# Matmul with subtraction on one core: runs of 16 m tiles, 36 longer transfers, an eighth VectorE pair, shared semaphores, and the last wait behind the section's exit

## Chip, cores, metric

One core of one Trainium2 chip. The metric is the device time of one execution in microseconds (us); a kernel's time is the median of its runs. Most of the argument is about the span that the profiler sees, some 1.8 us shorter than the time, and about moments in it, counted from its start.

## The reference

```python
batch, m, k, n = 16, 512, 1024, 768          # x [16,512,1024], weight [1024,768], sub_value [16,512,768], float32
def reference(x, weight, sub_value):
    return (np.matmul(x, weight) - sub_value).astype(np.float32)
```

That is 64 m tiles of 128 rows. Bytes to move: x 33.6 MB, weight 3.1, sub_value 25.2, output 25.2, together 87.03 MB.

## The kernel before

ScalarE casts a tile of x to fp16; PE transposes it (as pairs of fp16 in one 32-bit word), ScalarE evacuates the transpose, and PE multiplies it with the weight; VectorE subtracts in place in the ring that holds sub_value, from which the output leaves. For seven pairs of tiles VectorE transposes instead of PE. One queue (SP) issues all transfers, in the order of a list. A list entry is kind, first m tile, number of m tiles; `x` loads x, `s` sub_value, `w` a quarter of the weight, `o` stores output.

```python
S = 8                                       # m tiles in a run
NX, NSO = 16, 32                            # slots in the ring of x, in the ring of sub_value/output
ON_DVE = frozenset(range(18, 60, 6))        # first tiles of the pairs that VectorE transposes
TRANSFERS = [
    ('x', 0, 1), ('w', 0, 1), ('x', 1, 1), ('w', 1, 1), ('x', 2, 1), ('w', 2, 1),
    ('w', 3, 1), ('x', 3, 2), ('s', 0, 1), ('x', 5, 3), ('s', 1, 3), ('x', 8, 3),
    ('s', 4, 4), ('x', 11, 5), ('s', 8, 8), ('x', 16, 8), ('x', 24, 3), ('s', 16, 8),
    # ... cut ...
    ('x', 56, 8), ('s', 56, 8), ('o', 32, 8), ('o', 40, 8), ('o', 48, 8), ('o', 56, 4),
    ('o', 60, 2), ('o', 62, 1), ('o', 63, 1),
]
# partition p of a run holds S rows that follow each other, one for each m tile:
x_s = x_flat.rearrange("(s p j) k -> s p j k", p=P, j=S)
# ... cut: in issue(), for each entry once its waits can be named ...
sem = tc.alloc_semaphore(f"{kind}{at}")     # a semaphore for each transfer
sp.add(lambda here=here, there=there: nc.sync.dma_start(out=here, in_=there), waits, (sem, 16))
# ... cut: at the end, inside the section that all engines run in ...
for t in range(n_mt):
    if t == 0 or landed["o", t] is not landed["o", t - 1]:
        nc.sync.wait_ge(landed["o", t], 16)
```

A transfer that takes n m tiles of a run moves n consecutive rows for each of the 128 partitions; neighbouring partitions lie S rows apart in memory.

Of the kernel before, what the change touches and what calls it, by code (L numbers as in the profile page):

```python
# [10 lines left out]
F32 = mybir.dt.float32  # L11
F16 = mybir.dt.float16

S = 8
NX, NSO = 16, 32
N16, NXT, NPT, NPO = 4, 5, 2, 3
N16P, NXTP = 2, 2
# [2 lines left out]
LEAD_DVE = 7  # L20
PER = 4
HEAD = 3
ON_DVE = frozenset(range(18, 60, 6))
LOOP = None

TRANSFERS = [
    ('x', 0, 1), ('w', 0, 1), ('x', 1, 1), ('w', 1, 1), ('x', 2, 1), ('w', 2, 1),
    ('w', 3, 1), ('x', 3, 2), ('s', 0, 1), ('x', 5, 3), ('s', 1, 3), ('x', 8, 3),
    ('s', 4, 4), ('x', 11, 5), ('s', 8, 8), ('x', 16, 8), ('x', 24, 3), ('s', 16, 8),
    ('x', 27, 5), ('o', 0, 8), ('s', 24, 8), ('x', 32, 8), ('s', 32, 8), ('o', 8, 8),  # L30
    ('x', 40, 8), ('s', 40, 8), ('x', 48, 8), ('o', 16, 8), ('o', 24, 8), ('s', 48, 8),
    ('x', 56, 8), ('s', 56, 8), ('o', 32, 8), ('o', 40, 8), ('o', 48, 8), ('o', 56, 4),
    ('o', 60, 2), ('o', 62, 1), ('o', 63, 1),
]


# [66 lines left out]
def kernel(  # L103
# [7 lines left out]
    nc = tc.nc  # L111
# [7 lines left out]
    n_mt = M_TOT // P  # L119
# [3 lines left out]

    x_s = x_flat.rearrange("(s p j) k -> s p j k", p=P, j=S)
    sub_s = sub_flat.rearrange("(s p j) n -> s p j n", p=P, j=S)
    out_s = out_flat.rearrange("(s p j) n -> s p j n", p=P, j=S)
    w_c = weight.rearrange("(c p r) n -> c p r n", p=P, r=2)

    ctx.enter_context(tc.tile_critical(no_gpsimd_drain=True))  # L129

    def sbuf(name, shape, dtype):
        return ctx.enter_context(nc.sbuf_tensor(name, shape, dtype)).ap()
# [18 lines left out]
    counter = {}  # L151
# [4 lines left out]
    def count(name):  # L156
        so_far[name] += 1
        return (counter[name], 1)
# [23 lines left out]
    landed = {}  # L182
    cast_at, evac_at, pair_at, turn_at, mul_at, finish_at, w_at = {}, {}, {}, {}, {}, {}, {}
# [4 lines left out]
    def take(pool_name, n, mi):  # L188

        b = used[pool_name] % n  # L190
        used[pool_name] += 1
        slot[pool_name, mi] = b
        before = holder.get((pool_name, b))
        holder[pool_name, b] = mi
        return b, before
# [3 lines left out]
    todo = list(TRANSFERS)  # L199
    done = {"w": set(), "x": set(), "s": set(), "o": set(), "cast": set(), "finish": set()}  # L200
    staged = {}

    def issue():
        while todo:
            kind, at, n = todo[0]
            span = set(range(at, at + n))
            old = {t - NX if kind == "x" else t - NSO for t in span}
            need, by = {
                "w": (set(), "o"),
                "x": ({t for t in old if t >= 0}, "cast"),  # L210
                "s": ({t for t in old if t >= 0}, "o"),
                "o": (span, "finish"),
            }[kind]
            if not need <= done[by]:
                return
            todo.pop(0)
            done[kind] |= span
            sem = tc.alloc_semaphore(f"{kind}{at}")
            if kind == "w":

                first = NSO - 2 * (n_c - at)
                st = so_ring[:, first : first + 2]
                sp.add(lambda st=st, at=at: nc.sync.dma_start(out=st, in_=w_c[at]), then=(sem, 16))  # L223
                for r in range(2):
                    dve.add(
                        lambda at=at, r=r, st=st: nc.vector.tensor_copy(out=w_sb[:, at, r], in_=st[:, r]),  # L226
                        waits=[(sem, 16)], then=count("w"),
                    )
                    staged[first + r] = so_far["w"]
                w_at[at] = so_far["w"]  # L230
                continue
            ring, size, view = {
                "x": (x_ring, NX, x_s), "s": (so_ring, NSO, sub_s), "o": (so_ring, NSO, out_s)
            }[kind]
            here = ring[:, at % size : at % size + n]
            there = view[at // S][:, at % S : at % S + n]
            waits = []
            if kind == "x" and need:
                waits.append((counter["cast"], max(cast_at[t] for t in need)))
            if kind == "s":  # L240
                for t in need:
                    waits.append((landed["o", t], 16))
                for t in span:
                    if t % NSO in staged:
                        waits.append((counter["w"], staged.pop(t % NSO)))
            if kind == "o":
                waits.append((counter["finish"], max(finish_at[t] for t in need)))
            for t in span:
                landed[kind, t] = sem
            if kind == "o":  # L250
                here, there = there, here
            sp.add(lambda here=here, there=there: nc.sync.dma_start(out=here, in_=there), waits, (sem, 16))  # L252

    def cast(mi):
        assert mi in done["x"]
        done["cast"].add(mi)
        x_in = x_ring[:, mi % NX]
        first = mi - mi % 2
        waits = [(landed["x", mi], 16)]
        if first in ON_DVE:  # L260
            if mi == first:
                b, before = take("x16p", N16P, mi)
                if before is not None:
                    waits.append((counter["pair"], pair_at[before]))
            to = x16p_b[:, slot["x16p", first], mi - first]
        else:
            b, before = take("x16", N16, mi)
            if before is not None:
                waits.append((counter["turn"], turn_at[before]))
            to = x16_b[:, b]  # L270
        act.add(lambda: nc.scalar.copy(out=to, in_=x_in), waits, count("cast"))  # L271
        cast_at[mi] = so_far["cast"]
        issue()
# [27 lines left out]
    def transposes_dve(mi):  # L301

        x16 = x16p_b[:, slot["x16p", mi]].bitcast(F32).rearrange("p j (c q) -> p (j c) q", c=n_c)
        blocks = [(a, b) for a in range(P // Q) for b in range(P // Q)]

        def one(n, a, b):
            def f():
                waits = []
                if n == 0:
                    d, before = take("xtp", NXTP, mi)  # L310
                    waits.append((counter["cast"], cast_at[mi + 1]))
                    if before is not None:
                        waits.append((counter["mul"], mul_at[before + 1]))
                xt = xtp_b[:, slot["xtp", mi]].bitcast(F32).rearrange("p j (c m) -> p (j c) m", c=n_c)
                last = n == len(blocks) - 1
                dve.add(lambda: nc.vector.transpose(  # L316
                    xt[b * Q : (b + 1) * Q, :, a * Q : (a + 1) * Q],
                    x16[a * Q : (a + 1) * Q, :, b * Q : (b + 1) * Q],
                ), waits, count("pair") if last else None)
                if last:  # L320
                    pair_at[mi] = so_far["pair"]
            return f
        return [one(n, a, b) for n, (a, b) in enumerate(blocks)]

    def matmuls(mi, c):
        first = mi - mi % 2
        on_dve = first in ON_DVE
        waits = []
# [26 lines left out]
    def finish(mi):  # L355
        assert mi in done["s"]
        done["finish"].add(mi)
        o = so_ring[:, mi % NSO].rearrange("p (h n) -> p h n", h=2)
        po = po_b[:, slot["po", mi]]
        dve.add(lambda: nc.vector.tensor_tensor(  # L360
            out=o, in0=po[:, :, :NS], in1=o, op=mybir.AluOpType.subtract
        ), [(landed["s", mi], 16), (counter["mul"], mul_at[mi])], count("finish"))
        finish_at[mi] = so_far["finish"]
        issue()

# [15 lines left out]
    def lead(mi):  # L381
        return LEAD_DVE if mi - mi % 2 in ON_DVE else TA + CA

# [8 lines left out]
    idle(5)  # L392
    matmuls(0, 0)
    cast(1)
    transpose_tile(1)
    idle(4)
# [25 lines left out]
    for mi in range(HEAD, n_mt):  # L422
# [3 lines left out]
        t = mi + TA  # L426
        tr = transposes(t) if t < n_mt and t - t % 2 not in ON_DVE else []
        for c in range(n_c):
# [6 lines left out]
        finish(mi)  # L435
        if mi + LEAD_DVE - 1 in ON_DVE:
            waiting += transposes_dve(mi + LEAD_DVE - 1)
# [5 lines left out]

    for q in (sp, act, dve, pool):
        q.emit(q.ops)
    for t in range(n_mt):
        if t == 0 or landed["o", t] is not landed["o", t - 1]:
            nc.sync.wait_ge(landed["o", t], 16)
    if LOOP:
        first, size, times = LOOP  # L450
        pe.emit(pe.ops[: marks[first]])
        ends = [marks[first + size * n] for n in range(times + 1)]
        pe.emit_loop([pe.ops[a:b] for a, b in zip(ends, ends[1:])])
        pe.emit(pe.ops[ends[-1] :])
    else:
        pe.emit(pe.ops)


# [28 lines left out]
```

## Time and profile before

| | before |
|---|---|
| time, median of the first four runs | 211.37 us (211.04 to 211.59) |
| span of the profiled run | 209.36 us |
| PE busy / DMA engines busy | 95% / 97.8% |
| PE's last matmul ends | 204.41 us |
| eighth transfer (x3, x4) landed on all engines | 17.55 us |
| last output landed | 207.74 us |
| from there to the end of the span | 1.62 us |

The last four rows are read from the trace's instruction and landing times. One view more is needed later, the waits of PE from 24.3 us on. Its columns are: who waited, for whom, us in total, times, the longest.

```profile
PE po_b L175 <- ACT xt_b L296: 1.5, 1, 1.5
PE pt_b L289 <- ACT x_b L271: 1.4, 1, 1.4
PE po_b L175 <- DVE xtp_b L316: 0.3, 1, 0.3
```

The wait of the first line is at 57 us (that of the second ended at 24.1 us, as the window begins): the cast of tile 18 stands in ScalarE's order and waits for x16 to x23, which land at 56.56 us; the evacuation that PE needs stands behind it. So a late load shows as PE waiting for ScalarE.

### The profile page before, as it was taken

How to read it: one execution, taken by the hardware profiler on the slowest of the kernel's cores; microseconds unless marked ns; L12 is line 12 of the kernel's file. 1: busy time of each engine (PE TensorE's matmuls, PEld its weight loads, DVE VectorE, ACT ScalarE, POOL GpSimd, SP SyncE). 2: the span in 40 equal slices, each digit the busy share in tenths (PEclk: the TensorE clock that was granted, in tenths of full speed). 3: DMA queues.
4: the chain of work that ended last, by engine and by line, in shares of the span. 5: the costliest groups of instructions: out<-in, count | busy, mean ns of one | idle time of the engine just before them, and what ended most of it. 6: DMA issues, size and time to landing. Idle time of an engine off the chain costs nothing.

```text
span 209.4 us, 2456 instructions
## 1 busy us (share of the span) xinstructions
PE 198.4 (95%) x1250; PEld 80.4 (38%) x738; DVE 114.0 (54%) x186; ACT 112.9 (54%) x115; POOL 0.7 (0%) x6
## 2 busy tenths in 40 slices
PE   7998799999979999999999999999999999999990
PEld 2432244444333344344344334434434433444430
DVE  0242235106149849929956965992994795332231
ACT  2555665676396274655727629455572750765410
POOL 1000000000000000000000000000000000000000
PEclk9999999999999999999999999999999999999998
DMA  6999999999999999999999999999999999999994
GB/s 200 417 427 425 427 432 434 441 438 423 401 448 417 452 412 429 452 432 424 421 427 452 415 437 448 407 424 446 423 435 441 426 423 426 427 434 432 427 383 171
DMA packets 5626, 87.17 MB, mean 416 GB/s; under 512 B 624, under 2 KB 624, under 8 KB 2032
## 3 DMA queue, kind: packets, MB, share of 16 engines
q1 hardware_dynamic: 5616, 87.03, 97.8%
q8 instruction: 7, 0.11, 0.2%
q14 instruction: 3, 0.02, 0.0%
HBM read 61.87 MB, written 25.17 MB: 416 GB/s over the span
## 4 chain that ended last, share of the span: by engine, by line
PE 80%; DMA 6%; DVE 5%; ACT 4%; SPq 2%; issue 1%; ACTq 0%
PE po_b L175 71%; PE pt_b L289 10%; DMA x_ring<-in_x_dram 6%; DVE xtp_b L316 3%; ACT x_b L271 2%; ACT xt_b L296 1%; DVE so_ring L360 1%; SPq L223 1%; SPq L252 1%; ACT x16p_b L271 0%; SPq L482 0%; ACTq L56 0%; SPq L129 0%
## 5 line engine op out<-in xcount | busy, mean ns | idle before, releaser
L175 PE MATMUL po_b<-w_sb,xt_b 128*128 128x384 f16 x800 | 145.7, 326 | 1.5 <-ACT xt_b L296 1.5
L360 DVE TENSOR_TENSOR so_ring<-po_b,so_ring 128x768 f32<-128x768 f32 x64 | 60.7, 956 | 60.5 <-PE po_b L175 40.2
L296 ACT COPY xt_b<-pt_b 128x1024 f16<-128x1024 f16 x50 | 50.6, 1012 | 73.8 <-PE pt_b L289 73.1
L340 PEld LDWEIGHTS <-xt_b 128*128 128x128 f16 x400 | 39.2, 98 | 58.4 <-issue 52.9
L316 DVE STREAM_TRANSPOSE xtp_b<-x16p_b 32x256 f32<-32x256 f32 x112 | 48.8, 436 | 19.3 <-ACT x16p_b L271 17.4
L289 PE MATMUL pt_b<-ident,x_b 128*128 128x128 f32 x200 | 52.3, 274 | 2.7 <-ACT x_b L271 2.4
L271 ACT CAST x_b<-x_ring 128x1024 f16<-128x1024 f32 x50 | 51.6, 1048 | 5.9 <-DMA x_ring<-in_x_dram 5.9
L289 PEld LDWEIGHTS pt_b<-ident,x_b 128*128 128x128 f32 x200 | 27.6, 141 | 46.3 <-issue 40.4
L175 PE MATMUL po_b<-w_sb,xtp_b 128*128 128x384 f16 x224 | 42.9, 326 | 0.3 <-DVE xtp_b L316 0.3
L271 ACT CAST x16p_b<-x_ring 128x1024 f16<-128x1024 f32 x14 | 14.6, 1046 | 6.8 <-DMA x_ring<-in_x_dram 6.8
L340 PEld LDWEIGHTS <-xtp_b 128*128 128x128 f16 x112 | 11.0, 98 | 13.2 <-issue 11.2
L377 PE MATMUL po_b<-idle_x,idle_w 128*128 128x512 f16 x25 | 8.5, 496 | 1.5 <-DVE idle_x L371 1.5
L226 DVE CAST w_sb<-so_ring 128x768 f16<-128x768 f32 x8 | 4.1, 556 | 10.6 <-DMA so_ring<-in_weight_dram 10.6
L377 PEld LDWEIGHTS po_b<-idle_x,idle_w 128*128 128x128 f16 x25 | 3.0, 122 | 5.2 <-issue 3.0
L271 ACT ACT_TABLE_LOAD x1 | 1.3, 1283 | 0.9 <-SPq L129 0.9
L370 DVE MEMSET idle_w<- 128x64 uint32 x1 | 0.1, 112 | 1.0 <-SPq L129 1.0
L390 PE MATMUL po_b<-idle_x,idle_w 128*128 128x512 f16 x1 | 0.4, 379 | 0.0
L164 POOL TENSOR_SCALAR_AFFINE_SELECT ident<-ident 128x128 f32<-128x128 f32 x1 | 0.3, 292 | 0.1
L371 DVE MEMSET idle_x<- 128x256 uint32 x1 | 0.3, 272 | 0.0
L163 POOL MEMSET ident<- 128x128 f32 x1 | 0.2, 206 | 0.5 <-SPq L129 0.5
L390 PEld LDWEIGHTS po_b<-idle_x,idle_w 128*128 128x128 f16 x1 | 0.1, 98 | 0.2 <-issue 0.2
L471 POOL MEMSET const-bfloat16-1.0<- 128x1 bf16 x1 | 0.1, 102 | 0.0
(3 smaller groups left out, 0.3 us busy)
## 6 DMA issues: line engine op xcount, KB each, us to landing
so_ring<-in_sub_value_dram SPq DMA_DIRECT2D x7, 3072.0 KB, 24.3
out_dram<-so_ring SPq DMA_DIRECT2D x7, 3072.0 KB, 31.2
x_ring<-in_x_dram SPq DMA_DIRECT2D x5, 4096.0 KB, 22.7
x_ring<-in_x_dram SPq DMA_DIRECT2D x2, 2560.0 KB, 26.2
x_ring<-in_x_dram SPq DMA_DIRECT2D x3, 1536.0 KB, 22.4
so_ring<-in_weight_dram SPq DMA_DIRECT2D x4, 768.0 KB, 8.7
x_ring<-in_x_dram SPq DMA_DIRECT2D x3, 512.0 KB, 6.3
so_ring<-in_sub_value_dram SPq DMA_DIRECT2D x1, 1536.0 KB, 26.3
```

The costliest lines, as they stand in the source:

```text
L175: return nc.tensor.add_instruction(mybir.InstMatmult(name=nc.get_next_instruction_name(), engine=full.engine, ins=list(full.ins), outs=lis ...
L223: sp.add(lambda st=st, at=at: nc.sync.dma_start(out=st, in_=w_c[at]), then=(sem, 16))
L226: lambda at=at, r=r, st=st: nc.vector.tensor_copy(out=w_sb[:, at, r], in_=st[:, r]),
L252: sp.add(lambda here=here, there=there: nc.sync.dma_start(out=here, in_=there), waits, (sem, 16))
L271: act.add(lambda: nc.scalar.copy(out=to, in_=x_in), waits, count("cast"))
L289: pe.add(lambda: nc.tensor.transpose(words, from_, ident), waits, count("turn") if last else None)
L296: act.add(lambda: nc.scalar.copy(out=xt_b[:, d], in_=pt_b[:, b]), waits, count("evac"))
L316: dve.add(lambda: nc.vector.transpose(xt[b * Q : (b + 1) * Q, :, a * Q : (a + 1) * Q], x16[a * Q : (a + 1) * Q, :, b * Q : (b + 1) * Q],), ...
L340: pe.add(lambda weights=weights: nc.tensor.ldweights(weights, tile_position=(0, 0)), [w for w in waits if w[0] in ready])
L360: dve.add(lambda: nc.vector.tensor_tensor(out=o, in0=po[:, :, :NS], in1=o, op=mybir.AluOpType.subtract), [(landed["s", mi], 16), (counter[ ...
L377: lambda: nc.tensor.matmul(po_b[:, NPO - 1, 0], idle_w, idle_x, start=True, stop=True),
L390: pe.add(lambda: nc.tensor.matmul(po_b[:, NPO - 1, 0], idle_w, idle_x, start=True, stop=True), [(counter["ident"], 2)])
```

## The change

Its intent: fewer and longer transfers (runs of 16 tiles allow up to 16 tiles in one), less work for PE (an eighth pair on VectorE), fewer semaphores (called lanes; a lane is used again when its transfer is known to be done, and in the trace the 36 transfers use 16: ten carry one transfer each, six carry the other 26), and an exit of the section that doesn't wait for the last output.

```diff
-S = 8
+S = 16
-ON_DVE = frozenset(range(18, 60, 6))
+ON_DVE = frozenset(range(12, 60, 6))
 TRANSFERS = [
     ('x', 0, 1), ('w', 0, 1), ('x', 1, 1), ('w', 1, 1), ('x', 2, 1), ('w', 2, 1),
-    ('w', 3, 1), ('x', 3, 2), ('s', 0, 1), ('x', 5, 3), ('s', 1, 3), ('x', 8, 3),
-    ('s', 4, 4), ('x', 11, 5), ('s', 8, 8), ('x', 16, 8), ('x', 24, 3), ('s', 16, 8),
     ... cut ...
+    ('w', 3, 1), ('x', 3, 2), ('x', 5, 1), ('s', 0, 2), ('x', 6, 4), ('s', 2, 3),
+    ('x', 10, 4), ('s', 5, 4), ('s', 9, 7), ('x', 14, 2), ('x', 16, 6), ('s', 16, 5),
+    ('x', 22, 10), ('s', 21, 11), ('o', 0, 16), ('x', 32, 6), ('s', 32, 5), ('x', 38, 10),
+    ('s', 37, 11), ('x', 48, 8), ('o', 16, 9), ('o', 25, 7), ('s', 48, 8), ('x', 56, 8),
+    ('s', 56, 8), ('o', 32, 16), ('o', 48, 8), ('o', 56, 5), ('o', 61, 2), ('o', 63, 1),
 ]
-            sem = tc.alloc_semaphore(f"{kind}{at}")
+            sem, value = lane((kind, at))      # a lane is used again once all its transfers are known to be done
     ... cut: the waits use (sem, value) ...
-    for t in range(n_mt):
-        if t == 0 or landed["o", t] is not landed["o", t - 1]:
-            nc.sync.wait_ge(landed["o", t], 16)
+    for one in left:
+        if one is not last:
+            nc.sync.wait_ge(one["sem"], one["value"])
+    section.close()
+    with tc.tile_critical(sync_engine=mybir.EngineType.SP, no_gpsimd_drain=True):
+        nc.sync.wait_ge(last["sem"], last["value"])
```

## The prediction

> **What bounds the kernel now.** I read the page's busy shares first, then the DMA part, then windows of the span, then the chain of work that ended last, and then the timeline at the end together with the trace's landing times.
>
> ```profile
> PE 198.4 (95%) x1250; PEld 80.4 (38%) x738; DVE 114.0 (54%) x186; ACT 112.9 (54%) x115; POOL 0.7 (0%) x6
> ...
> DMA packets 5626, 87.17 MB, mean 416 GB/s; under 512 B 624, under 2 KB 624, under 8 KB 2032
> ...
> q1 hardware_dynamic: 5616, 87.03, 97.8%
> ...
> HBM read 61.87 MB, written 25.17 MB: 416 GB/s over the span
> ```
>
> Two candidates stand side by side: PE is busy 95% of 209.4 us, and the 16 DMA engines 97.8%. Each looks like the bound, so I ask how each stands in stretches of the span. The columns of the next view are the stretch, its length, the busy us of PE, PEld, DVE, ACT and POOL, PE's clock, the DMA share (1.00 is 16 engines busy) and GB/s.
>
> ```profile
> 5.00:24.00 19.00, 16.45 (x91) 6.38 (x63) 5.07 (x9) 10.96 (x12) 0.00 (x0) 1.00 1.02 423
> 24.00:60.00 36.00, 34.31 (x223) 14.97 (x135) 11.02 (x12) 22.01 (x24) 0.00 (x0) 1.00 1.01 432
> 60.00:75.00 15.00, 14.71 (x96) 5.64 (x53) 12.62 (x22) 8.12 (x10) 0.00 (x0) 1.00 1.01 431
> 75.00:200.00 125.00, 125.00 (x811) 50.91 (x467) 82.92 (x139) 70.13 (x72) 0.00 (x0) 1.00 1.00 429
> 200.00:205.00 5.00, 4.41 (x28) 1.17 (x12) 1.61 (x3) 0.31 (x1) 0.00 (x0) 1.00 0.91 382
> 205.00:209.40 4.40, 0.00 (x0) 0.00 (x0) 0.41 (x1) 0.00 (x0) 0.00 (x0) 0.82 0.34 136
> ```
>
> The DMA engines are full from 5 to 200 us, without a hole: never under 1.00. PE has small holes before 75 us (19.00 - 16.45, 36.00 - 34.31, 15.00 - 14.71 us) and none after. Which of the two sets the end is read from the last microseconds.
>
> ```profile
> 199.21 5.21 PE po_b L175 x32
> 204.42 0.02 issue
> 204.45 0.96 DVE so_ring L360
> ```
>
> The chain of work puts the end down to PE: last matmul at 204.42, the last subtraction until 205.41, the last output transfer issued at 205.43. The trace's landing times show the DMA side. A transfer lands in 16 shares, one per DMA engine. The last but one (one m tile) has its first share at 204.97 and its last at 206.83 us: some engines run 1.9 us behind others. The last transfer, issued at 205.43, lands from 207.57 to 207.74. Its first packets start at about 206.25, that is 0.8 us after the issue; an engine needs 8 packets of 122 ns for it. The most backward engine read its last packet of the transfer before at about 206.38, so it went straight on. So both bounds coincide at the end to about 0.1 us: the leading DMA engines waited for PE, and the last one never waited. A kernel like this gets shorter only if PE and the DMA work both do.
>
> **What the Trainium skill says.** "DMA: Bandwidth & Descriptors", § Bandwidth, puts the ceiling at 16 ports x 32 B x 850 MHz = 435 GB/s; this trace agrees, with 429 to 432 GB/s in the full stretches. Its § Why small descriptors are slow names a fixed cost per packet. I fit it from this trace: median packet times are 122 ns for 3,072 B, 234 for 6,144, 462 for 12,288, 912 for 24,576 and 1,213 for 32,768. The slope is (1213 - 122) / 29,696 B = 0.0367 ns/B, or 27.2 GB/s per engine, 436 for 16; the intercept is 122 - 3,072 x 0.0367 = 9 ns. A semaphore packet takes 9 ns more. The same page's § Latency and other measured facts warns that rows at large power-of-two pitches can slow transfers, but has 512 KiB still at full rate; the pitch here goes from 32 to 64 KiB (x), so I expect nothing, and no run yet shows it. "Perfetto Trace Analysis", § DMA Instruction, says that the semaphore update waits until the write is confirmed, surprisingly long for HBM; here the last output's landing lags its last packet by about 0.35 us.
>
> **The change part by part.**
>
> *Fewer and longer transfers.* 39 become 36, and bytes stay the same: 87.03 MB. Every transfer is 128 data packets and 16 semaphore packets: 39 x 144 = 5,616, the count of q1. After: 36 x 144 = 5,184. On one engine that is 3 x 8 x 9 + 3 x 9 = 243 ns less, out of 205.4 us of work (1.97 to 207.37). Runs of 16 m tiles only allow a partition's row to be up to 49,152 B; they don't change bytes, and at 32,768 B the fixed 9 ns are under 1% of a packet already. DMA path: -0.24 us.
>
> *An eighth pair on VectorE* (tiles 12 and 13). The chain shows the steady pace:
>
> ```profile
> 82.98 5.85 PE po_b L175 x36
> ...
> 100.33 5.85 PE po_b L175 x36
> ```
>
> Six m tiles take 17.35 us: 96 matmuls at 5.85 / 36 = 0.1625 are 15.60, and the 16 transposes of the four tiles on PE are the rest, 1.75, or 0.109 each. Two tiles less on PE: 8 x 0.109 = 0.88 us. VectorE gains 16 transposes of 436 ns, 7.0 us, and ScalarE loses two evacuations of 1,012 ns; both are at 54%, so there is room.
>
> ```profile
> L316 DVE STREAM_TRANSPOSE xtp_b<-x16p_b 32x256 f32<-32x256 f32 x112 | 48.8, 436 | 19.3 <-ACT x16p_b L271 17.4
> ```
>
> *The order of loads.* The first eight transfers are the same, so the head up to 17.55 us is. Then I add up the new list at the measured pace (1.23 us per m tile of x, 0.93 of s or o, and 1.1 us for a backward engine from 28 us on). x16 to x21 land at 54.4 us; in the kernel before, x16 to x23 land at 56.56. That landing is what PE lost 2.5 us to before, at 56.8, 59.1 and 70.1 us, because the cast of tile 18 stands in front of others on ScalarE (it waited 3.5 us). The landing comes 2.1 us earlier and PE's demand 0.9 us earlier, so some 1 us of the loss stays. PE needs 61 x 16 x 0.1625 + 43 x 4 x 0.109 = 177.4 us from 24.1 us on: 201.5 without stalls, with them 202.3 to 203 rather than 204.4.
>
> But this is not the end any more: the last output, issued at about 204, lands when the backward engine is through with everything before it. That engine's work is 0.24 us shorter, if the queue never runs dry. I checked the late issues for that: o0 to o15 must land (about 96 us) before s32 can be issued, with 7.3 us of x32 to x37 still queued; o16 to o24 (148) before s48, with 6.4 us queued; the last big outputs are ready 4 to 20 us before the queue reaches them. First packets follow an issue by 0.8 us, so none of these empties it. Last landing: 207.74 - 0.24 = 207.5 us.
>
> *The end.* From the last landing to the end of the span the kernel before takes 209.36 - 207.74 = 1.62 us: in the trace about 0.5 us of it is SP collecting the other engines at the section's exit, 0.05 its last drain, the rest the two barriers with the clearing of semaphores (0.33 us) between. The new version passes that exit while the last transfer is still in flight (the other five shared semaphores are waited for first, the last of them some 0.95 us earlier), and then has a small exit with SP alone, for which I allow 0.15 us. So -0.35 us. Fewer semaphores (6 for transfers, not 39) may shorten the clearing; I count 0.05 us.
>
> Sum: -0.24 - 0.35 - 0.05 = -0.64, so 211.55 - 0.65 = 210.9 us.
>
> **The rivals.**
>
> *PE sets the end.* Then PE's 1.4 to 2 us would come through and, with the exit, the time would be about 209.5 us. For it: the chain of work names PE for 80% of the span. Against: DMA shares of 1.00 and more in every window to 200 us, and the backward engine without a gap at the end.
>
> *Long transfers make PE wait.* A tile can be cast only when its whole transfer has landed. s2 to s4 land at 28.4 to 29.4 us where the subtraction of tile 2 must be over by 29.6 us, x22 to x31 at 71.2 us, x32 to x37 at 103 us where PE wants tile 32 at 103.4. Each may cost PE about 1 us. PE has some 1.4 us to spare before the DMA end, so one such wait is hidden; three would show, 211.5 to 213 us.
>
> *The queue runs dry or the longer pitch is slower.* With outputs of 16 tiles the loads that reuse their room come in lumps. A hole of some us goes straight into the time. A rate 1% lower would be 2 us: 213. The trace before has 159 ns for 4,096 B at the 32 KiB pitch, full rate, so I hold this unlikely.
>
> *Luck of the instruction fetches.* Seven fetches of 16 KB land each on one DMA engine and cost it 0.6 to 1.1 us. If another engine gets them, the most backward one is 0.5 us less or more behind.
>
> **Range and chances.** The sum says 210.9. The fetches and the spread of the runs before (211.04 to 211.59) give 0.5 us to both sides; PE as the bound would go to 209.5, lumps to 213. Eight times in ten: 210.0 to 211.8 us. Faster by 2% means under 207.3, which is 4.2 us less with the same bytes at a rate that is at the ceiling: 2%. Slower by 2% means over 215.8: only with a hole in the queue or a slower pitch: 3%. Within 2%: 95%.
>
> **What would show it.** Right: 5,184 packets in q1 at a share near 98%; PE transposes x192, VectorE transposes x128; PE's last matmul at 202 to 203 us and yet the last landing at 207.3 to 207.6; end of span some 1.2 us after it, not 1.6; PE's wait near 57 us shorter. Wrong: a DMA share under 0.98 in a window between 5 and 200 us (a dry queue), a median packet time off the line 9 + 0.0367 per byte (pitch), new PE waits after 75 us that move its end past 204.4, or a last landing that follows PE's end by the same 3.3 us as before (then PE is the bound). The prediction fails if the DMA end moves by more than 1 us.

## The result

| | before | after |
|---|---|---|
| time, median | 211.37 us | 211.03 us (210.93 to 211.30) |
| ratio | | 0.9987 (0.9969 to 1.0006) |
| span | 209.36 | 209.15 |
| PE's last matmul ends | 204.41 | 203.10 |
| eighth transfer landed | 17.55 | 17.91 |
| last output landed | 207.74 | 207.84 |
| from there to the end | 1.62 | 1.31 |

A ratio is the mean time of one kernel's fast runs over that of the other's of the same rounds, so it is not quite the ratio of the medians. The changed kernel was run again, with more rounds: 0.9974 (0.9958 to 0.9991) and 0.9970 (0.9939 to 1.0001). Its medians were 0.34, 0.47 and 0.48 us below those of the kernel before. One of the three intervals leaves out "no change". Over all runs, 16 of the changed kernel and 37 of the kernel before, the medians differ by 0.40 us and the means by 0.52, since four runs of the kernel before are over 212 us. So there is a gain, of about 0.4 to 0.5 us, where 0.65 was predicted.

The page of the changed kernel: the busy shares, the packets and the queue, then the two transposing groups.

```profile
PE 197.7 (95%) x1242; PEld 79.4 (38%) x730; DVE 120.8 (58%) x202; ACT 111.0 (53%) x113; POOL 0.7 (0%) x6
...
DMA packets 5194, 87.17 MB, mean 417 GB/s; under 512 B 576, under 2 KB 576, under 8 KB 1984
...
q1 hardware_dynamic: 5184, 87.03, 97.9%
...
L339 DVE STREAM_TRANSPOSE xtp_b<-x16p_b 32x256 f32<-32x256 f32 x128 | 55.8, 436 | 16.0 <-ACT x16p_b L294 13.9
...
L312 PE MATMUL pt_b<-ident,x_b 128*128 128x128 f32 x192 | 50.2, 274 | 2.6 <-ACT x_b L294 2.4
```

The counts are as they had to be: 432 packets fewer, 16 transposes more on VectorE and 8 fewer on PE. PE is less busy, the DMA engines are not. The same windows as in the prediction:

```profile
5.00:24.00 19.00, 16.79 (x91) 6.52 (x63) 5.94 (x10) 10.64 (x11) 0.00 (x0) 1.00 1.02 420
24.00:60.00 36.00, 34.30 (x223) 14.43 (x132) 18.43 (x30) 22.13 (x24) 0.00 (x0) 1.00 1.03 437
60.00:75.00 15.00, 15.00 (x98) 5.89 (x55) 11.44 (x20) 7.85 (x9) 0.00 (x0) 1.00 0.96 414
75.00:200.00 125.00, 124.99 (x809) 50.46 (x465) 82.67 (x139) 69.06 (x71) 0.00 (x0) 1.00 1.00 431
200.00:205.00 5.00, 3.10 (x20) 0.78 (x8) 1.92 (x2) 0.00 (x0) 0.00 (x0) 1.00 0.90 383
```

The 0.96 between 60 and 75 us looks like the hole in the queue that the prediction named as a sign against it. It is not one. The packets at its first border (40,960 B each) last 1.5 us, and such a view gives a packet to one window, hence 1.03 in the window before. Cut exactly at the borders, the trace's packet times give 1.003 and 1.001 for these two windows. The end of the chain of work:

```profile
197.90 5.21 PE po_b L175 x32
203.12 0.02 issue
203.14 0.96 DVE so_ring L383
```

PE ends 1.3 us earlier than before, yet the last output lands 0.1 us later. Issued at 204.13, it took 3.7 us to land, where it had taken 2.3: its first engines are done at 206.27, its last, after everything else in its queue, at 207.84. Before, its 16 shares lay within 0.17 us.

PE's waits from 24.3 us on have moved:

```profile
PE pt_b L312 <- ACT x_b L294: 1.4, 1, 1.4
PE po_b L175 <- DVE so_ring L383: 1.3, 1, 1.3
```

The wait at 57 us is gone. A new one of 1.3 us is at 30 us, and the chain of work around it shows why:

```profile
6.70 23.54 DMA so_ring<-in_sub_value_dram
30.24 0.03 issue
30.27 0.02 DVEq L55
30.29 0.04 issue
30.33 0.97 DVE so_ring L383
31.30 0.04 issue
31.34 0.81 PE po_b L175 x4
```

The load of s2 to s4 lands at 30.24 us, VectorE then subtracts tile 2, and only then has PE room for its next sums. That it lands so late is chance: 15 of its 16 shares are in by 28.75 us, and only the last is 1.49 us behind them. Instructions come in over the same DMA engines (more on this at `mix`): a fetch of 1.06 us that begins at 28.08 us, and the packet right after it, 0.49 us longer than its like, are about that time. The profile after_third has the same (15 shares by 28.68, the last at 30.24, a wait of 1.3 us), but after_again has not. There all shares are in by 29.14 us, and its waits are others, of 0.3 us at 68 us and 0.4 us at 104 us (the 1.4 us in the first line ended before the window, as above):

```profile
PE pt_b L312 <- ACT x_b L294: 1.8, 2, 1.4
PE po_b L175 <- DVE xtp_b L339: 0.3, 1, 0.3
```

No wait at 57 us comes back there, without the wait at 30 us: x16 to x21, landed at 54.54 us (54.87 in the first profile), some 2 us sooner than x16 to x23 before, are no longer late.

### The profile page after: what moved, and what is told of

It is laid out like the page before. It is cut to its first block, busy times and chain, and to the rows that moved or that the text cites. A ratio compares the mean times of both kernels' runs of the same rounds, so it can differ in the third digit from the quotient of the medians.

```text
span 209.2 us, 2454 instructions
## 1 busy us (share of the span) xinstructions
PE 197.7 (95%) x1242; PEld 79.4 (38%) x730; DVE 120.8 (58%) x202; ACT 111.0 (53%) x113; POOL 0.7 (0%) x6
## 4 chain that ended last, share of the span: by engine, by line
PE 82%; DMA 11%; SPq 3%; DVE 1%; issue 0%; DVEq 0%
PE po_b L175 74%; DMA so_ring<-in_sub_value_dram 11%; PE pt_b L312 9%; SPq L275 2%; SPq L239 1%; DVE so_ring L383 1%; SPq L511 0%; DVEq L55 0%; SPq L129 0%
## 5 line engine op out<-in xcount | busy, mean ns | idle before, releaser
L175 PE MATMUL po_b<-w_sb,xt_b 128*128 128x384 f16 x768 | 138.8, 326 | 1.3 <-DVE so_ring L383 1.3
L319 ACT COPY xt_b<-pt_b 128x1024 f16<-128x1024 f16 x48 | 48.6, 1012 | 57.8 <-PE pt_b L312 56.8
L339 DVE STREAM_TRANSPOSE xtp_b<-x16p_b 32x256 f32<-32x256 f32 x128 | 55.8, 436 | 16.0 <-ACT x16p_b L294 13.9
L363 PEld LDWEIGHTS <-xt_b 128*128 128x128 f16 x384 | 37.6, 98 | 58.4 <-issue 55.1
L294 ACT CAST x_b<-x_ring 128x1024 f16<-128x1024 f32 x48 | 49.5, 1047 | 16.0 <-DMA x_ring<-in_x_dram 15.9
L312 PE MATMUL pt_b<-ident,x_b 128*128 128x128 f32 x192 | 50.2, 274 | 2.6 <-ACT x_b L294 2.4
L175 PE MATMUL po_b<-w_sb,xtp_b 128*128 128x384 f16 x256 | 49.1, 326 | 0.0
L312 PEld LDWEIGHTS pt_b<-ident,x_b 128*128 128x128 f32 x192 | 26.5, 141 | 44.4 <-issue 38.9
L294 ACT CAST x16p_b<-x_ring 128x1024 f16<-128x1024 f32 x16 | 16.7, 1046 | 13.4 <-DMA x_ring<-in_x_dram 13.4
L363 PEld LDWEIGHTS <-xtp_b 128*128 128x128 f16 x128 | 12.6, 98 | 14.8 <-issue 12.6
```

What stands on the lines that cost most here:

```text
L175: return nc.tensor.add_instruction(mybir.InstMatmult(name=nc.get_next_instruction_name(), engine=full.engine, ins=list(full.ins), outs=lis ...
L294: act.add(lambda: nc.scalar.copy(out=to, in_=x_in), waits, count("cast"))
L312: pe.add(lambda: nc.tensor.transpose(words, from_, ident), waits, count("turn") if last else None)
L319: act.add(lambda: nc.scalar.copy(out=xt_b[:, d], in_=pt_b[:, b]), waits, count("evac"))
L339: dve.add(lambda: nc.vector.transpose(xt[b * Q : (b + 1) * Q, :, a * Q : (a + 1) * Q], x16[a * Q : (a + 1) * Q, :, b * Q : (b + 1) * Q],), ...
L363: pe.add(lambda weights=weights: nc.tensor.ldweights(weights, tile_position=(0, 0)), [w for w in waits if w[0] in ready])
```

## The experiments

The theory to test: the DMA engines' work sets the last landing in the changed kernel, with PE about 1 us ahead; in the kernel before, the two are level; what is gained comes mostly from the exit. The main rival: PE sets the end, as the chain of work has it in both kernels. "Against before" is the mean of the runs less that of the kernel before in the same rounds.

| run | against before, us | ratio (95%) | PE ends | eighth landing | last landing | to the end |
|---|---|---|---|---|---|---|
| b_exit | -0.19 | 0.9990 (0.9967-1.0012) | 204.45 | 17.40 | 207.78 | 1.46 |
| b_pair60 | -0.41 | 0.9979 (0.9956-1.0002) | 203.76 | 17.26 | 207.30 | 1.62 |
| b_pairs6 | +0.89 | 1.0041 (1.0017-1.0064) | 205.37 | 17.34 | 208.70 | 1.62 |
| b_run16 | +0.60 | 1.0027 (0.9998-1.0056) | 206.28 | 17.70 | 209.60 | 1.62 |
| after_again | -0.53 | 0.9974 (0.9958-0.9991) | 203.03 | 18.30 | 207.94 | 1.31 |
| a_less_s | -1.43 | 0.9932 (0.9916-0.9948) | 203.06 | 17.83 | 206.87 | 1.31 |
| b_less_s | -0.22 | 0.9991 (0.9974-1.0008) | 204.25 | 17.22 | 207.58 | 1.62 |
| a_pairs7 | +0.22 | 1.0010 (0.9982-1.0038) | 204.77 | 17.66 | 209.47 | 1.31 |
| mix | -0.65 | 0.9970 (0.9936-1.0004) | 201.55 | 17.47 | 208.46 | 1.30 |
| after_third | -0.65 | 0.9970 (0.9939-1.0001) | 203.14 | 17.87 | 207.83 | 1.31 |
| a_pairs7_again | +0.54 | 1.0027 (0.9982-1.0071) | 203.00 | 17.76 | 207.72 | 1.31 |
| a_exit_old | -0.21 | 0.9991 (0.9964-1.0018) | 202.62 | 17.76 | 208.04 | 1.47 |

The right half is from the one profiled run of each, so it explains that run; the left half is from five or six.

### Less DMA work, the same PE work

Both kernels, wrong on purpose: the last m tile of sub_value is not loaded, so the last m tile of the output is wrong. The changed kernel, unedited, was run beside them.

```diff
             here = ring[:, at % size : at % size + n]     # before this line, in both kernels:
+            if kind == "s" and at + n == n_mt:
+                n -= 1
```

> The changed kernel itself, as the base of the other three of this call. Expected 0.3 to 0.5 us shorter than the kernel before (ratio 0.998 to 0.9985), last landing 207.4 to 207.9 us, PE's last matmul at 203.0 to 203.2 us.

> The changed kernel, wrong on purpose: the load of the last m tile of sub_value (0.39 MB, 0.93 us of every DMA engine) is left out, so the last m tile of the output is wrong. Theory (DMA work sets the end and PE has about 1 us to spare): the last landing comes 0.8 to 0.95 us earlier, and so does the end. Rival (PE sets the end): time unchanged within 0.15 us, for PE has the same to do.

> The same edit to the kernel before, wrong on purpose too. Theory (there PE is level with the DMA work, so that less DMA work alone gains nothing): last landing 207.6 to 207.75, time shorter by 0 to 0.15 us. If DMA alone set the end before, 0.8 to 0.95 us shorter.

The changed kernel lost 210.85 - 209.95 = 0.90 us (means of the runs), just about the 0.93 us of DMA work taken away, while PE did the same; the last landing came 0.97 us earlier than in the first profile of the changed kernel (206.87 and 207.84). The chain of work of its shortened version ends

```profile
197.86 5.21 PE po_b L175 x32
203.07 0.02 issue
203.09 0.96 DVE so_ring L385
```

within 0.1 us of where it does in the three profiles of the changed kernel: PE is not what moved. The rival, that PE sets the end of the changed kernel, falls, and with it the reading of the chain of work, which names PE there too. The chain follows semaphores back from the last instruction; it cannot show that the last transfer lay in a queue behind others.

The kernel before lost 0.22 us with the same edit, a quarter as much; I expected 0 to 0.15, and the interval (-0.55 to +0.17) leaves no change possible but not the 0.8 to 0.95 of the rival. In its profile the last output lands 3.33 us after PE's last matmul (204.25 to 207.58), the distance of the unedited kernel too (204.41 to 207.74): there PE decides.

### PE work added and removed in the kernel before

```diff
-ON_DVE = frozenset(range(18, 60, 6))
+ON_DVE = frozenset(range(18, 66, 6))     # b_pair60: eight pairs, tiles 60 and 61 added
+ON_DVE = frozenset(range(18, 54, 6))     # b_pairs6: six pairs, tiles 54 and 55 back on PE
```

> The kernel before with an eighth pair on VectorE, tiles 60 and 61, so that PE has 0.88 us less to do after its last wait. Theory (DMA work sets the end): PE's last matmul at 203.5 instead of 204.4 us, last landing still 207.6 to 207.75, time shorter by 0 to 0.15 us. Rival (PE sets the end, as the chain of work says): time shorter by 0.8 to 0.9 us.

> The kernel before with six pairs on VectorE instead of seven (tiles 54 and 55 go back to PE): PE has 0.88 us more to do. Theory that in the kernel before both bounds coincide at the end to 0.1 us: PE's last matmul at 205.3, the last landing at 208.5 to 208.7, time longer by 0.75 to 0.9 us. If PE had slack there, time longer by less than 0.3 us.

Six pairs: +0.89 us, for 0.88 us of PE work more. Eight: PE's last matmul at 203.76 instead of the expected 203.5, because of a wait of 0.5 us at 48 us that the kernel before had not, and the last landing at 207.30. Its distance from PE's end grew from 3.33 to 3.54 us, so the queue has begun to decide. The gain of 0.41 us is more than the 0 to 0.15 expected, and its interval (-0.93 to +0.04) holds both and the rival's 0.8 to 0.9 too; so here the time decides nothing, and what follows rests on one profile. Part of it in the profiled run is an early start: counted from the eighth landing, the last landing is 190.04 us away, against 190.19 in the kernel before, 0.15 us less. So of the 0.88 us taken from PE (its end came 0.65 us earlier) at most half came through: the DMA engines' end is only 0.1 to 0.2 us away from PE's.

### The eighth pair taken back from the changed kernel

```diff
-ON_DVE = frozenset(range(12, 60, 6))
+ON_DVE = frozenset(range(18, 60, 6))     # a_pairs7 and a_pairs7_again
```

> The changed kernel with the eighth pair (tiles 12 and 13) taken back to PE. Theory (PE has about 1 us to spare): PE's last matmul moves by up to 0.9 us to about 204, the last landing stays within 0.1 us of that of the changed kernel, and the time too. Rival (PE sets the end): 0.7 to 0.9 us longer than the changed kernel.

> The changed kernel with seven pairs again, because its first profile fell in a run with a stretch at 77 to 79 us in which the packets of all DMA engines took 1.9 to 2.9 us instead of 1.25. Theory (PE has slack): without such a stretch the last landing is 189.6 to 190.1 us after the eighth and the fast runs are those of the changed kernel within 0.15 us; if long packets come again in some runs, the median is higher and the lowest run still equal. Rival (PE sets the end): even the lowest run is 0.7 us longer.

By the times, this test did not settle what it was for. In the mean the seven pairs are 0.75 us longer than the changed kernel beside them in the first, as the rival has it, and 1.20 in the second. The six times of the first are 210.82, 210.85, 211.24, 211.88, 212.28 and 212.55 us; of the second 211.01, 211.11, 211.48, 212.00, 213.34 and 213.52. The lowest are near those of the changed kernel (210.56 to 211.30 in its 16 runs), the high ones are not, and the changed kernel has none such; but the kernel before has (212.48 and 212.85), so they don't belong to this edit alone. In the first profile some twenty packets of s21 to s31 (33,792 B) took 1.7 to 2.9 us between 76.6 and 80 us instead of 1.25. The last landing was then 191.80 us after the eighth; in the second profile, without such a stretch, 189.96. There PE's last matmul was at 203.00, as early as with eight pairs: its waits had changed more than its work (0.5 us in all from 24.3 us on, against 1.3 in the first profile of the changed kernel and 2.4 in a_pairs7). In both profiles the last output lands 4.7 us after PE's last matmul, not 3.3, so by the sign that the prediction named PE did not set the end of either. The lowest runs are 0.19 and 0.45 us above the lowest of the changed kernel beside them, less than the rival's 0.7; why seven pairs have the long runs stays open. That PE has slack rests on a_less_s and on these distances.

### The exit, in both directions

```diff
 # b_exit: the kernel before, with the two lines of section.close() and the second section of the change,
 #         and only the last output waited for there; 39 semaphores as they were
 # a_exit_old: the changed kernel with
-    section.close()
-    with tc.tile_critical(sync_engine=mybir.EngineType.SP, no_gpsimd_drain=True):
-        nc.sync.wait_ge(last["sem"], last["value"])
+    nc.sync.wait_ge(last["sem"], last["value"])
```

> The kernel before with the exit alone changed: only the last output is waited for after the section's exit. Theory (DMA work sets the last landing, the new exit takes about 0.3 us off what follows it): last landing unchanged at 207.7 us, span end 1.25 to 1.45 us after it instead of 1.62, time 0.2 to 0.35 us shorter, and this is nearly all of what the change gains. The clearing of semaphores stays at 331 ns, since there are still 39 of them for transfers. Rival (the exit costs as much as it hides): same time.

> The changed kernel with all outputs waited for inside the section, as before, and its shared semaphores kept. From the exit alone in the kernel before (1.62 to 1.46 us from the last landing to the end) and from the clearing (331 to 203 ns): end 1.45 to 1.50 us after the last landing instead of 1.31, time 0.1 to 0.2 us longer than the changed kernel, which five rounds will hardly tell from the same.

With these and the two kernels, all four combinations have a profile. From the last landing to the end of the span: old exit and 39 transfer semaphores 1.62 us, new exit and 39 1.46, old exit and 16 1.47, both changes 1.31. The first is 1.62 in all five profiles of its kind, the last 1.31 in all six with 16 semaphores. The new exit is worth 0.16 us, the fewer semaphores 0.15. The second is seen as one instruction, GpSimd's clearing of the range of semaphores: 331 ns in every profile with 39, 203 with 16. The timed difference is -0.19 us for b_exit, just short of the theory's 0.2 to 0.35, with an interval (-0.70 to +0.25) that holds no change too, so the worth of the exit rests on the profiles; a_exit_old is 0.45 us longer than the changed kernel on the same chip (211.33 and 210.88, means), more than the 0.17 that the exit explains. In its profile the last landing is 190.28 us after the eighth, 0.32 later than beside it; the cause of that I don't know.

### The pitch of the rows alone

```diff
-S = 8
+S = 16        # the kernel before, its list of transfers unchanged
```

> The kernel before with runs of 16 m tiles and its own list of transfers: the rows of one transfer lie 64 KiB (x) and 48 KiB (s, o) apart instead of 32 and 24, nothing else changes. In the profile after, the eighth transfer landed at 17.91 us, 0.36 later than before. If the pitch costs this, the eighth landing is again near 17.9 and the time about 0.3 us longer; if it is chance of the start, the landing is within the spread of the other runs and the time the same within 0.15 us.

The eighth landing is at 17.70. Over all profiles, the six with x in runs of 8 have it from 17.22 to 17.55 us (mean 17.37), the eight with runs of 16 from 17.66 to 18.30 (mean 17.85). The two sets don't overlap, so it is not chance. The loss lies in the first two loads of x: x0 lands at 4.61 to 4.93 us with runs of 8 and 4.91 to 5.29 with 16; x1 lands 1.27 to 1.29 us after the transfer ahead of it with 8 and 1.29 to 1.70 with 16. The third, x2, takes 1.24 to 1.29 us in both. So rows 64 KiB apart cost about half a microsecond once, near the start, and nothing that shows later in median packet times: 159 ns for 4,096 B in both kernels, 1,213 for 32,768.

The time grew by 0.60 us in the mean, with an interval (-0.04 to +1.18) that holds no change too. The profiled run is the longest of the six (213.31 us); the other five average 0.34 us more than the kernel before, about what the start costs. What made the profiled one so long is an after-effect. The longest wait of PE in this run:

```profile
PE po_b L175 <- ACT xt_b L296: 1.8, 1, 1.8
```

Two windows of it, with the columns as above:

```profile
54.00:60.40 6.40, 4.47 (x29) 1.79 (x17) 0.96 (x1) 3.17 (x4) 0.00 (x0) 1.00 0.98 416
60.40:63.80 3.40, 3.40 (x13) 1.22 (x7) 2.64 (x5) 2.54 (x3) 0.00 (x0) 0.50 1.01 434
```

And the kernel before in the second of them:

```profile
60.40:63.80 3.40, 3.40 (x24) 1.49 (x14) 3.24 (x7) 2.84 (x4) 0.00 (x0) 1.00 0.99 426
```

x16 to x23 landed at 57.21 instead of 56.56 us. The wait for them grew from 1.5 to 1.8 us, and after it PE's clock (the column before the DMA share) was at half for 3.41 us: 13 matmuls instead of 24. PE ended 1.9 us later. In this run a load 0.65 us late put PE's end back by three times that. Whether the clock drops turns on little: b_pairs6 waited 1.6 us at the same place (57.05 us) and kept its clock.

### A version meant to beat both

`mix` keeps the runs of 16 from tile 16 on, but lays the first 16 tiles in runs of 8 and loads them by the first 15 entries of the old list; o0 to o15 leave in two transfers; the eighth pair is at 60 and 61.

```diff
-S = 16
+S, SHORT, FIRST = 16, 8, 16
-ON_DVE = frozenset(range(12, 60, 6))
+ON_DVE = frozenset(range(18, 66, 6))
+            run = SHORT if at < FIRST else S
+            view = near[kind] if at < FIRST else view     # near: the views of x, sub_value, output with j=SHORT
-            there = view[at // S][:, at % S : at % S + n]
+            there = view[at // run][:, at % run : at % run + n]
```

> A candidate to beat both: the changed kernel with the first 16 m tiles laid in runs of 8 and loaded by the old list's first 15 transfers, and with the eighth pair at tiles 60 and 61 in place of 12 and 13. Theory (the wider pitch costs 0.3 to 0.7 us in the first two loads of x, everything after the eighth landing is DMA work): eighth landing at 17.2 to 17.6 us as in all runs of 8, last landing about 189.9 us after it, 207.0 to 207.5; end 1.31 us later; time 0.3 to 0.6 us shorter than the changed kernel on the same chip. If the late eighth landings were chance, it is the same as the changed kernel.

> The changed kernel once more, as the base of this call. Eighth landing at 17.6 to 18.3 us, PE's last matmul at 203.0 to 203.3, last landing 189.6 to 190.0 us after the eighth, time 0.3 to 0.5 us shorter than the kernel before.

It does not beat the changed kernel: both means are 210.88 us. Its start is as early as expected (17.47), and PE ends at 201.55, 1.6 us sooner than in the changed kernel. Its six times fall apart: 210.25, 210.34, 210.63, 210.67, and 211.56 and 211.84. The profiled run is the last of these, and the landing times show what was slow in it. Instructions are fetched over the same 16 DMA engines: in its span seven blocks of 16,384 B on one queue, which by their number I take for PE's, and three of 8,192 B on another. A fetch holds up one engine. In the transfer that ends landing at 161.46 us the shares lie within 2.39 us, and the last engine is 0.36 us behind the next. In the following one, x56 to x63 (168.78 to 172.12 us), it is 1.30 us behind and the spread is 3.34 us, which stays: the shares of the last transfer spread over 3.27 us. Between the two lies a fetch of 8,192 B, at 168.37 us for 0.31 us, and right after it a packet 0.55 us longer than its like, together most of the 0.94 us lost; the 16,384 B fetch at 177.44 us came after it and made the spread no wider. The last landing is 190.98 us after the eighth, not 189.9. In the three profiles of the changed kernel the spread of the shares grows at the first 16,384 B fetch by 0.65, 1.34 and 1.54 us, in one and the same program, while that fetch and the longer packet after it cost nearly the same each time (1.06 + 0.49, 1.10 + 0.47 and 1.06 + 0.50 us): so what changes is which engine is hit, one that was ahead or one that was behind. The low four runs average 210.47 us, but a kernel has to be judged with all its runs.

## Why the prediction was right, and where its steps were off

The interval held, and so did the mechanism: PE's gain was hidden behind the DMA engines' work, and a small rest came from the exit and from clearing fewer semaphores. By its steps:

- **Both bounds level before.** Shown for more PE work, which cost its full length (b_pairs6). Less of either alone gained less than half of it or a quarter (b_pair60, b_less_s); these two gains are within the noise of the times, and the landing times carry them. More DMA work alone was not tried.
- **PE ahead after the change.** PE's last matmul was predicted at 202.3 to 203 and came at 203.0 to 203.1. The way there was another, and in part luck. I had put the loss before at 2.5 us, where my own windows show 1.98 (36.00 - 34.31 and 15.00 - 14.71). The rest of the wait at 57 us that I had kept in the sum is gone. The wait for s2 to s4, which I had only among the rivals, at "about 1 us", took 1.3 in two of the three profiles, where an instruction fetch fell on that load; in the third a later start (24.8 instead of 24.4 us) and 0.7 us of other waits came to the same end. a_less_s shows that PE doesn't decide any more.
- **DMA path, -0.24 us.** This term was mis-sized, because of its neighbour: "the pitch here goes from 32 to 64 KiB (x), so I expect nothing". The fewer packets are there: from the eighth landing to the last, 190.19 us became 189.93, -0.26, though part of that is PE's share in the end before; against b_pair60, where the queue has begun to decide (190.04), the three profiles are 0.11, 0.40 and 0.08 us shorter. But the eighth landing itself came 0.36 us later in that pair of profiles, 0.48 in the mean of all. The last landing was thus +0.10 us, not -0.24. That the head stays as it is because its eight transfers are the same overlooked that their rows lie farther apart.
- **The exit, -0.35, and the semaphores, -0.05.** Together 0.32 were measured, in other parts: 0.16 and 0.15. From the last landing to GpSimd's first step of the last barrier the traces have 0.68 us with the old exit and 0.52 with the new, so the second, small exit of SP cost more than the 0.15 us that I had allowed. For the semaphores I had counted too little gain, and from a wrong number: I took six for transfers, and the trace has 16.
- **Luck of the fetches.** Named as a rival at 0.5 us. In mix a fetch on the engine that was already last cost about 0.9 us, and the wait at 30 us comes and goes with a fetch.
- **Luck of the base.** The 210.9 us was counted from 211.55, the median of the three runs then known; a fourth made it 211.37. From there the predicted gain gives 210.7, and the 211.03 measured is 0.3 us above it, not 0.1.

In the first pair of profiles the measured terms are +0.10 - 0.32 = -0.22 us, against -0.64 predicted; the spans differ by 0.21. The medians differ by more, 0.34 to 0.48 us, for in the kernel before the profiled run was one of its shorter ones (211.14 us).

## What to carry to other kernels

When two bounds end within 0.1 us of each other, work added to one (here PE) costs its full length and work taken from one gains little more than the distance to the other; take a known piece of work from each in turn (here one load, here one pair) before optimizing, and don't trust the chain of work where the last transfer may have stood in a queue. A reordering of rows in memory that leaves sizes and order alone can still move the first loads, so compare landing times of the start, not only packet times. Below about 0.5 us, look at the spread of runs and at where the instruction fetches fall before crediting an edit.

## What the Trainium skill lacked or had wrong

- "DMA: Bandwidth & Descriptors", § Latency and other measured facts, tells of row pitches from 512 KiB up, in copies between HBM tensors; it has 207 GB/s at 512 KiB against the 214 it calls full, which the prediction read as full rate. Here a pitch of 64 instead of 32 KiB cost the first two loads of x some 0.5 us (eighth landing at 17.85 instead of 17.37 us in the mean), and did not show in the median packet times of later ones; the page has no such start effect.
- "TensorE: Matmul & The Clock Gate", § What's actually happening, has the clock go down after an idle window of about 3.4 us. The length of the slow stretch agrees (3.41 us at half clock in b_run16), but the 3.41 us before it, from 56.96 us, were not idle: PE was busy for 43% of them, with one wait of 1.8 us and one of 0.1. The clock's changes lie whole multiples of 3.41 us apart in every profile; of all such stretches after the clock first rose, until PE's work ends, that one is the least busy, and the next, 51% in b_pairs6, left the clock alone.
- "Runtime: NRT & Kernel Launch", § Instruction fetch mechanics, gives blocks of 16 KiB (the trace agrees: seven fetches of 16,384 B) and calls their cost mostly hidden. In a kernel whose DMA engines are full, the first such block widened the spread of a transfer's shares by 0.65 to 1.54 us, and the slowest engine sets the last landing. No page says which engine is hit.
- No page has the time of the one instruction that clears a kernel's own semaphores at its end, by their number: 331 ns with 39 for transfers, 203 ns with 16.
